# A DeepNorm decoder layer on one core: the gates gb and rg and the two branch projections as seven block products in one stretch, and the rotary tables beside HGRN2

## The chip, the core and the metric

The kernel runs on one core of a Trainium2 chip. The time is that of the device in microseconds (us), from a run of the whole program; lower is better. Before the change the median of three runs is 2408.48 us (2407.49 to 2409.2). The engines of the core are called as the profile calls them: PE is TensorE (PEld its weight loads), DVE is VectorE, ACT is ScalarE, POOL is GpSimd, SP is SyncE, which here only issues transfers (DMAs). POOL issues transfers too, on a queue of its own.

## The reference, cut to what matters

One layer, 1024 tokens of width 1024, everything in float32. `u` is the scaled and shifted input; one wide projection `w_in` gives the inputs of two recurrences and four gates; `rg`, `ga`, `gb` and the projections `w_pa` and `w_pb` are the places of this change.

```python
u = x * (1.0 + scale1) + shift1
hq, hf, hi, hg, rq, rk, rv, rg, ga, gb = jnp.split(u @ w_in[l], split_at, axis=-1)
ya = _hgrn2(hq, hf, hi, hg, lower_bounds[l]) @ w_pa[l]
yb = _retention(rq, rk, rv, rg, positions) @ w_pb[l]
y = (jax.nn.sigmoid(ga) * ya + jax.nn.sigmoid(gb) * yb) @ w_o[l]
x = _layer_norm(DEEPNORM_ALPHA * x + (1.0 + gate1) * y, ln1_g[l], ln1_b[l])
u = x * (1.0 + scale2) + shift2
h = jnp.square(jax.nn.relu(u @ w_up[l] + b_up[l]))
y = h @ w_down[l] + b_down[l]
x = _layer_norm(DEEPNORM_ALPHA * x + (1.0 + gate2) * y, ln2_g[l], ln2_b[l])
...
def _retention(q, k, v, g, positions):
    theta = ROPE_BASE ** (-jnp.linspace(0.0, 1.0, RET_DK // 2, dtype=f32))
    ang = positions.astype(f32)[:, :, None, None] * theta
    cos, sin = jnp.cos(ang), jnp.sin(ang)
    ...
    o = _head_norm(_from_chunks(o), centered=True).reshape(B, S, RET_WIDTH)
    return (o * jax.nn.silu(g.astype(f32))).astype(g.dtype)
```

Here `g` of the retention is `rg` (2048 columns); `gb` and `ga` have 1024 columns, `w_pa` is 1024 x 1024 and `w_pb` 2048 x 1024.

## The kernel before

**Matmuls.** Every float32 operand is split into a high and a low part (`split`, L170 to 172: ScalarE rounds into `wh`, `hh` or `uh`, VectorE subtracts into `wl`, `hl` or `ul`). A product is then three matmuls, `mm3` (L176, L177, L178): high by high, high by low, low by high. Weights come as 512 KB pieces through one stream in the order of a list of specs: SP loads a piece into one of three `raw` tiles, the split writes one of three pairs `wh`, `wl`, two pieces ahead of their use (`W`). SP's queue holds the stream and all other reads in program order, POOL's queue most writes.

**Order of the work.** Start (adaLN, `u` transposed into `uh`, `ul`); HGRN2 in four pairs of heads, each pair's dense projections woven with the recurrence of the one before, outputs stored to `oh_d`; the gate `ga` (to `ga_d`); `h_merge`, which reloads `oh_d`, projects it by `w_pa` and stores the gated result to `y1_d`, woven with `rotary`, which computes the tables of cosines and sines on VectorE and ScalarE; the retention, four heads one after the other (outputs to `or_d`); the gate `gb` (`gate_proj`, to `gb_d`); then for each head of the retention the gate `rg` (`r_merge_gate`: sigmoid, two products with the recurrence's output, split) and its part of the projection by `w_pb` (`r_merge_acc`, which adds into `y`, and for the last head multiplies by gb and adds y1); the output projection, `ffn_up`, `ffn_down`. A scheduler orders the instructions of each engine from this program order and their dependences.

**Seven block products.** `ffn_up` and `ffn_down` already use a form of Strassen's scheme (Winograd's): both matrices are cut into 2 x 2 blocks, and seven products q1 to q7 of sums of blocks replace eight. Sums of weight blocks are made in DRAM by transfers that POOL issues, copies and accumulating copies (`block_sums`, L196 and L197), eight for every part. They are paced by TensorE: `mm3` lets one go each time it has done `PREP` = 40 * 512 columns of matmuls, 42 matmuls of 512 columns (14 calls of `mm3`). Sums of blocks of the other matrix are made by VectorE. For `ffn_down` these are seven variants per tile, written by POOL to `hv_d` (1792 KB a write) and read back by SP into `hr` tiles (512 KB).

Of the kernel before, what the change touches and what calls it, by code (L numbers as in the profile page):

```python
# [58 lines left out]
B12_SLOT = 7  # L59
UP_ORDER = ("q1", "q5", "q6", "q2", "q7", "q3", "q4")  # L60
DN_ORDER = ("q1", "q5", "q6", "q3", "q7", "q2", "q4")
UP_STEPS = ([(q, p) for q in ("q1", "q2") for p in (0, 1)] +
            [(q, p) for p in (0, 1) for q in UP_ORDER if q not in ("q1", "q2")] +
            [(q, p) for p in range(2, 8) for q in UP_ORDER])
LAST = 4
PREP = 40 * 512
# [71 lines left out]
class Trunk:  # L138
# [48 lines left out]
    def block_sums(self, name, w, cut):  # L187


        nc = self.nc  # L190
        kh, nh = w.shape[0] // 2, w.shape[1] // 2
        part = (lambda a, p: a[:, nh // 8 * p:nh // 8 * (p + 1)]) if cut else (lambda a, p: a[kh // 8 * p:kh // 8 * (p + 1), :])
        w11, w12, w21, w22 = ([part(w[k * kh:(k + 1) * kh, n * nh:(n + 1) * nh], p) for p in range(8)]
                              for n in (0, 1) for k in (0, 1))
        s1, s2, s3, s4 = ([self.dp.tile(list(w11[0].shape), F32, name=f"{name}_s{j}_{p}") for p in range(8)] for j in range(1, 5))
        copy = lambda d, a: self.sums.append((0, lambda: nc.gpsimd.dma_start(d, a)))  # L196
        add = lambda late, d, a: self.sums.append((late, lambda: nc.gpsimd.dma_start(d, a, accum_op=ALU.add, max_dma_last_dim=8192)))  # L197
        for p in range(8):
# [103 lines left out]
    def dense_T(self, wh, wl, half, uh=None, ul=None, ks=range(KT), tag="d", k0=0):  # L302
        uh = uh or self.uh
        ul = ul or self.ul
        pd = self.ps(tag)
        sl = slice(half * 512, half * 512 + 512)
        ks = list(ks)
        for k in ks:
            self.mm3(pd, wh[:, k], wl[:, k], uh[k0 + k][:, sl], ul[k0 + k][:, sl], k == ks[0], k == ks[-1])
        return pd  # L310
# [71 lines left out]
    def start(self):  # L382
# [4 lines left out]
        self.uh = [self.up.tile([P, T], F32R, name=f"uh{k}") for k in range(KT)]  # L387
        self.ul = [self.up.tile([P, T], F32R, name=f"ul{k}") for k in range(KT)]
# [41 lines left out]
        def turn(k, hf):  # L430
# [11 lines left out]
            self.split(self.uh[k][:, sl], self.ul[k][:, sl], u32[k][:, sl])  # L442
# [8 lines left out]
        for k in range(KT):  # L451
# [3 lines left out]
            for hf in (0, 1):  # L455
# [4 lines left out]
                sl = slice(hf * 512, hf * 512 + 512)  # L460
                for (wh, wl), bk in zip(wt, banks):
                    self.mm3(bk[hf], wh[:, k], wl[:, k], self.uh[k][:, sl], self.ul[k][:, sl], k == 0, False)
        for j, ((wh, wl), bk) in enumerate(zip(wt, banks)):
            for hf in (0, 1):
                sl = slice(hf * 512, hf * 512 + 512)
                self.mm3(bk[hf], wh[:, k], wl[:, k], self.uh[k][:, sl], self.ul[k][:, sl], False, True)
# [48 lines left out]
    def h_values(self, p):  # L515
# [4 lines left out]
        for t in range(8):  # L520
            pd = self.ps("d", (P, 256))
            for k in range(KT):
                wh, wl = w[k // 4]
                tk = slice(t * P, (t + 1) * P)
                self.mm3(pd, self.uh[k][:, tk], self.ul[k][:, tk], wh[:, k % 4], wl[:, k % 4], k == 0, k == KT - 1)
# [119 lines left out]
    def h_pair_rec(self, p):  # L645
        for hd in (0, 1):
            for _ in self.h_rec(p, hd):
                self.tick()
                yield
# [16 lines left out]


    def h_merge(self):
        nc = self.nc
        oh, ol = [], []  # L670
        for e in range(KT):
            t = self.mp.tile([P, 1024], F32, tag="ohr", bufs=2, name=self.uid("ohr"))
            nc.sync.dma_start(t, self.oh_d[e])
            oh.append(self.mp.tile([P, T], F32R, name=f"oh{e}"))
            ol.append(self.mp.tile([P, T], F32R, name=f"ol{e}"))
            self.split(oh[e], ol[e], t)
        for m in range(KT):
            wh, wl = self.W(("pa", m // 2, m % 2))
            for hf in (0, 1):
                sl = slice(hf * 512, hf * 512 + 512)  # L680
                sg = self.mp.tile([P, 512], F32, tag="sga", bufs=2, name=self.uid("sga"))
                nc.sync.dma_start(sg, self.ga_d[m][:, sl])
                pd = self.dense_T(wh, wl, hf, oh, ol)
                y = self.mp.tile([P, 512], F32, tag="y1", bufs=2, name=self.uid("y1"))
                nc.vector.tensor_tensor(y, pd, sg, op=ALU.mult)
                nc.gpsimd.dma_start(self.y1_d[m][:, sl], y)
                yield


    def rotary(self):  # L690
# [29 lines left out]
        for s in range(T // W):  # L720
            cs = slice(s * W, (s + 1) * W)
            pi = self.rp.tile([P, W], I32, tag="rot_i", bufs=1, name=self.uid("rot"))
            nc.sync.dma_start(pi, self.i["positions"][0:1, cs].to_broadcast([P, W]))
            a, m, y, n = (self.rp.tile([P, W], F32, tag="rot_" + c, bufs=1, name=self.uid("rot")) for c in "amyn")
            V.tensor_copy(a, pi)
# [3 lines left out]
            V.scalar_tensor_tensor(a, m, -65536.0, a, op0=ALU.mult, op1=ALU.add)  # L729
            reduce(a, n)  # L730
            for c in q16[:2]:
                V.tensor_scalar(y, m, sgn * c, None, op0=ALU.mult)
                reduce(y, n)
                V.tensor_tensor(a, a, y, op=ALU.add)
            V.scalar_tensor_tensor(a, m, sgn * q16[2], a, op0=ALU.mult, op1=ALU.add)
            reduce(a, n)
            V.tensor_scalar(a, a, 3.1415925, -3.1415925, op0=ALU.min, op1=ALU.max)
            nc.scalar.activation(self.sin[:, cs], a, AF.Sin)
            nc.scalar.activation(y, a, AF.Sin, scale=0.5)
            V.tensor_tensor(y, y, y, op=ALU.mult)  # L740
            V.tensor_scalar(self.cos[:, cs], y, -2.0, 1.0, op0=ALU.mult, op1=ALU.add)
# [74 lines left out]
    def r_v(self, h, t, w):  # L816
        nc = self.nc
        pd = self.ps("d", (P, 256))
        tk = slice(t * P, (t + 1) * P)
        for k in range(KT):  # L820
            wh, wl = w[k // 4]
            self.mm3(pd, self.uh[k][:, tk], self.ul[k][:, tk], wh[:, k % 4], wl[:, k % 4], k == 0, k == KT - 1)
# [99 lines left out]
    def r_merge_gate(self, h, e, last):  # L922
        nc = self.nc
        wh, wl = self.W(("rg", h, e // 2, e % 2), ahead=0 if last else 1)
        on = self.mp.tile([P, T], F32, tag="onr", bufs=2, name=self.uid("onr"))
        nc.sync.dma_start(on, self.or_d[h][e * P:(e + 1) * P, :])
        oh = self.mp.tile([P, T], F32R, tag="moh", bufs=5, name=self.uid("moh"))
        ol = self.mp.tile([P, T], F32R, tag="mol", bufs=5, name=self.uid("mol"))
        for hf in (0, 1):
            sl = slice(hf * 512, hf * 512 + 512)  # L930
            pd = self.dense_T(wh, wl, hf)
            sg = self.gp.tile([P, 512], F32, tag="gate", bufs=2, name=self.uid("gate"))
            nc.scalar.activation(sg, pd, AF.Sigmoid)
            nc.vector.tensor_tensor(sg, sg, pd, op=ALU.mult)
            nc.vector.tensor_tensor(sg, sg, on[:, sl], op=ALU.mult)
            self.split(oh[:, sl], ol[:, sl], sg)
        return oh, ol

    def r_merge_acc(self, h, mp, os, halves, key, ahead):
        nc, V = self.nc, self.nc.vector  # L940
        wh, wl = self.W(key, k=4, ahead=ahead)
        for j in (0, 1):
            m = 2 * mp + j
            ms = slice(j * P, (j + 1) * P)
            for hf in halves:
                sl = slice(hf * 512, hf * 512 + 512)
                if h == RH - 1:
                    gb = self.mp.tile([P, 512], F32, tag="gbr", bufs=2, name=self.uid("gbr"))
                    nc.sync.dma_start(gb, self.gb_d[m][:, sl])
                    y1 = self.mp.tile([P, 512], F32, tag="y1r", bufs=2, name=self.uid("y1r"))  # L950
                    nc.sync.dma_start(y1, self.y1_d[m][:, sl])
                pd = self.ps("d")
                for e in range(4):
                    self.mm3(pd, wh[:, e, ms], wl[:, e, ms], os[e][0][:, sl], os[e][1][:, sl], e == 0, e == 3)
                ya = self.y[hf][:, m, :]
                if h == 0:
                    nc.scalar.activation(ya, pd, AF.Copy)
                else:
                    V.tensor_tensor(ya, ya, pd, op=ALU.add)
                if h == RH - 1:  # L960
                    V.tensor_tensor(ya, ya, gb, op=ALU.mult)
                    nc.gpsimd.tensor_tensor(ya, ya, y1, op=ALU.add)
# [113 lines left out]
    def variant(self, pool, q, src):  # L1076
        hi, lo = (pool.tile([P, 4, 512], F32R, tag=q + c, bufs=1, name=self.uid(q + c)) for c in "hl")
        for k in (0, 2):
            self.split(hi[:, k:k + 2], lo[:, k:k + 2], src[:, k:k + 2])
        self.act[q] = (hi, lo)  # L1080

    def variants(self, va, vb):

        V = self.nc.vector
# [386 lines left out]
```

## Time and profile before

Times are in us from the start of the profiled span; the columns are the busy times of the engines, the share of the 16 DMA engines and the bytes moved.

| What | time |
|---|---|
| median of three runs | 2408.48 |
| the profiled execution | 2407.94 |
| its span in the profile | 2405.9 |

| Stage | from : to | PE busy | DVE busy | ACT busy | DMA share | GB/s |
|---|---|---|---|---|---|---|
| start | 0 : 60 | 44.52 | 49.12 | 26.82 | 1.01 | 264 |
| HGRN2, end of the first dense part | 60 : 130 | 70.00 | 24.90 | 26.66 | 0.44 | 117 |
| HGRN2, a pair | 250 : 377 | 125.57 | 82.18 | 31.82 | 0.31 | 83 |
| last pair and ga | 505 : 632 | 123.06 | 88.46 | 32.91 | 0.45 | 135 |
| ffn_up | 1810 : 2087 | 277.00 | 137.50 | 157.78 | 0.59 | 204 |
| ffn_down | 2087 : 2406 | 308.50 | 190.88 | 118.25 | 0.63 | 208 |

The stages between 632 and 1810 stand in the prediction. An engine's busy time in a stage, against the stage's length, tells whether it could be the one that sets the pace; the DMA share counts the time that packets took on the 16 engines, so it can exceed 1 where they overlap.

### The profile page before, as it was taken

To read this page: it belongs to the slowest core of one execution; us is meant where nothing else is said; L and a number is where in the kernel's file an instruction comes from. 1 tells how busy PE (TensorE), PEld (TensorE's weight loads), DVE (VectorE), ACT (ScalarE), POOL (GpSimd) and SP (SyncE) were. 2 spreads that over 40 slices of the span, in tenths; PEclk is the share of its full clock that TensorE was granted. 3 is DMA by queue.
4 is the path that set the end of the run, shared out by engine and by line. 5 is a ranking of instruction groups with operands and counts; after the bars stand their busy time and mean duration, and the time that the engine had idled before them with its cause. 6 is when DMAs were issued, how large, how long until landed. Compare 5 with 4: busy or idle time off the path is not lost.

```text
span 2405.9 us, 31784 instructions
## 1 busy us (share of the span) xinstructions
PE 2360.5 (98%) x12434; PEld 2020.3 (84%) x12434; DVE 1383.8 (58%) x2578; ACT 826.5 (34%) x1363; POOL 252.1 (10%) x347
## 2 busy tenths in 40 slices
PE   7999999999999999999999999999999999999998
PEld 5898888887888989898998888887778888888886
DVE  8356667576766474656541324438776454544577
ACT  4322222222312334242432231223366555544332
POOL 0101111112120112111122000003100000000000
PEclk9999999999999999999999999999999999999999
DMA  9324233232875254444446545536424655866673
GB/s 264 104 73 105 62 81 86 80 97 88 242 216 154 54 147 109 123 131 102 131 128 196 154 114 132 140 97 227 158 96 162 215 186 190 298 219 193 212 245 137
DMA packets 223253, 357.65 MB, mean 149 GB/s; under 512 B 12040, under 2 KB 154112, under 8 KB 219008
## 3 DMA queue, kind: packets, MB, share of 16 engines
q1 hardware_dynamic: 186816, 229.32, 30.0%
q0 software_dynamic: 35968, 125.85, 19.5%
q8 instruction: 98, 1.61, 0.3%
q14 instruction: 51, 0.42, 0.1%
q10 hardware_dynamic: 320, 0.45, 0.1%
HBM read 292.65 MB, written 130.03 MB: 176 GB/s over the span
## 4 chain that ended last, share of the span: by engine, by line
PE 90%; DVE 5%; DMA 3%; issue 1%; ACT 1%; POOL 1%; ACTq 0%; SPq 0%; DVEq 0%; POOLq 0%
PE psd L177 22%; PE psd L176 22%; PE psd L178 22%; PE psa L581 3%; PE psb L871 3%; PE psc L176 2%; PE psc L177 2%; PE psc L178 2%; PE psa L177 2%; PE psa L178 2%; PE psa L176 2%; PE psc L858 2%; PE psb L176 1%; PE psb L177 1%; PE psb L178 1%
## 5 line engine op out<-in xcount | busy, mean ns | idle before, releaser
L172 DVE TENSOR_TENSOR wl<-raw,wh 128x512 fp32r<-128x512 f32 (+1 forms) x312 | 294.9, 955 | 325.5 <-ACT wh L171 295.7
L176 PE MATMUL psd<-uh,wh 128*128 128x512 f32 x1128 | 447.1, 397 | 0.0
L177 PE MATMUL psd<-ul,wh 128*128 128x512 f32 x1128 | 444.9, 394 | 0.4 <-DVE ul L172 0.4
L178 PE MATMUL psd<-uh,wl 128*128 128x512 f32 x1128 | 444.0, 394 | 0.0
L171 ACT ACTIVATE wh<-raw 128x512 fp32r<-128x512 f32 (+1 forms) x312 | 259.0, 840 | 493.7 <-PE psd L177 386.2
L177 PEld LDWEIGHTS psd<-ul,wh 128*128 128x128 f32 x1128 | 212.2, 188 | 41.9 <-DVE ul L172 1.5
L178 PEld LDWEIGHTS psd<-uh,wl 128*128 128x128 f32 x1128 | 212.1, 188 | 41.8
L176 PEld LDWEIGHTS psd<-uh,wh 128*128 128x128 f32 x1128 | 211.9, 188 | 41.4 <-ACT uh L171 0.7
L176 PE MATMUL psd<-wh,uh 128*128 128x256 f32 x768 | 221.6, 289 | 0.0
L177 PE MATMUL psd<-wl,uh 128*128 128x256 f32 x768 | 218.2, 284 | 0.0
L178 PE MATMUL psd<-wh,ul 128*128 128x256 f32 x768 | 218.0, 284 | 0.0
L176 PEld LDWEIGHTS psd<-wh,uh 128*128 128x128 f32 x768 | 147.1, 192 | 2.9 <-issue 2.6
L177 PEld LDWEIGHTS psd<-wl,uh 128*128 128x128 f32 x768 | 147.1, 192 | 0.3
L178 PEld LDWEIGHTS psd<-wh,ul 128*128 128x128 f32 x768 | 147.1, 192 | 0.0
L172 DVE TENSOR_TENSOR hl<-hr,hh 128x1024 fp32r<-128x1024 f32 x54 | 66.1, 1223 | 115.7 <-ACT hh L171 115.7
L171 ACT ACTIVATE hh<-hr 128x1024 fp32r<-128x1024 f32 x54 | 57.3, 1061 | 159.8 <-PE psb L177 73.0
L178 PE MATMUL psd<-moh,wl 128*128 128x512 f32 x256 | 99.9, 390 | 1.8 <-DVE wl L172 1.8
L176 PE MATMUL psd<-moh,wh 128*128 128x512 f32 x256 | 99.6, 390 | 0.4 <-ACT wh L171 0.4
L177 PE MATMUL psd<-mol,wh 128*128 128x512 f32 x256 | 99.9, 390 | 0.0
L588 DVE COPY_PREDICATED hS<-mask,psa 128x128 f32<-128x128 uint8 x288 | 77.1, 314 | 31.7 <-PE psa L581 28.9
L827 DVE SCALAR_TENSOR_TENSOR vl<-psd,cst,vh 128x256 fp32r<-128x256 f32 x64 | 30.8, 482 | 82.7 <-ACT vh L826 82.7
L581 PE MATMUL psa<-qp,k 128*128 128x192 f32 x384 | 72.2, 329 | 1.3 <-DVE k L557 1.3
(423 smaller groups left out, 4890.7 us busy)
## 6 DMA issues: line engine op xcount, KB each, us to landing
raw<-in_w_in SPq DMA_DIRECT2D x96, 512.0 KB, 4.3
hv_d<-hv POOLq DMA_DIRECT2D x16, 1792.0 KB, 9.3
hr<-hv_d SPq DMA_DIRECT2D x56, 512.0 KB, 5.5
up_s<-in_w_up POOLq DMA_DIRECT2D x48, 512.0 KB, 5.3
dn_s<-in_w_down POOLq DMA_DIRECT2D x48, 512.0 KB, 5.2
raw<-in_w_ada SPq DMA_DIRECT2D x32, 512.0 KB, 4.5
raw<-up_s SPq DMA_DIRECT2D x32, 512.0 KB, 3.8
raw<-dn_s SPq DMA_DIRECT2D x32, 512.0 KB, 4.7
```

The costliest lines, as they stand in the source:

```text
L171: self.nc.scalar.activation(hi, src, AF.Copy)
L172: self.nc.vector.tensor_tensor(lo, src, hi.bitcast(F32), op=ALU.subtract)
L176: r = mm(out, wh, uh, start=start, stop=False, skip_group_check=more)
L177: mm(out, wh, ul, start=False, stop=False, skip_group_check=more)
L178: l = mm(out, wl, uh, start=False, stop=stop, skip_group_check=more)
L581: nc.tensor.matmul(pa[:, c * 192:(c + 1) * 192].rearrange("p (b w r) -> p b w r", w=2, r=3 * sz), k[:, n * P:(n + 1) * P], mv, start=True, ...
L588: V.copy_predicated(dst, self.mask8[:, o:o + 128].rearrange("p (b two s) -> p b two s", two=2, s=sz), src)
L827: nc.vector.scalar_tensor_tensor(lo, pd, sc, hi.bitcast(F32), op0=ALU.mult, op1=ALU.subtract)
L858: mm(G[e], l[:, n % 2, es], r, start=n == 0 and i == 0, stop=i == 2, skip_group_check=n > 0)
L871: mm(po, l, r, start=i == 0, stop=i == len(pairs) - 1)
```

## The change

**What it does.** The gates gb and rg run as `gates()` right behind the retention, the projections pa and pb behind them as `merge()`, all four in seven block products. `h_merge` is gone from its place ahead of the retention. Their weights take 12 more parts in `block_sums` (2 for gb, 4 for rg, 2 for pa, 4 for pb, besides 8 each for up and dn), so 28 x 8 = 224 sum transfers in place of 128, and `PREP` goes from 40 * 512 to 24 * 512. `u` is kept in four blocks `ub`; `gates()` adds its high and low parts up again (`whole`) and forms the sums of blocks by `t_sums`, which `ffn_up` now shares. The outputs of the recurrences are read into `hv` tiles (`take`: `or_d` for rg, `oh_d` for pa), where rg's gate is multiplied in; their seven variants go by POOL to `av_d` (pa) and `pv_d` (pb) in writes of 1792 KB, and `merge()` reads them as `hr` like `ffn_down` does. The gates ga and gb and the first projection's result y1 are read in pieces of 256 KB (`fetch`). The rotary tables are computed by a generator that is advanced while HGRN2's pairs run, stored to `cos_d` and `sin_d`, and read again ahead of the retention.

```diff
-PREP = 40 * 512
+PREP = 24 * 512
+MERGE_ORDER = ("q1", "q2", "q6", "q7", "q5", "q4", "q3")
+GATE_STEPS = group_steps([("gb", p) for p in range(2)] + [("rg", p) for p in range(4)])
...
+    def product(self, q, name, p):
+
+        wh, wl = self.W((q, name, p), k=4)
+        ah, al = self.act[q]
...
+            for k in range(4):
+                self.mm3(s[tag], wh[:, k, gs], wl[:, k, gs], ah[:, k], al[:, k], first and k == 0, k == 3, not first)
+            yield s, j, s[tag]
...
+    def gate_block(self, s, name, j, n, k, src, sign):
+        nc, V = self.nc, self.nc.vector
+        if name == "gb":
+            r = self.o_tile() if src is s["X"] else src
+            nc.scalar.activation(r, src, AF.Sigmoid, scale=sign)
+            nc.gpsimd.dma_start(self.gb_d[4 * n + j][:, k * 512:k * 512 + 512], r)
+            return
+        r = self.o_tile()
+        nc.scalar.activation(r, src, AF.Sigmoid, scale=sign)
+        V.scalar_tensor_tensor(r, src, sign, r, op0=ALU.mult, op1=ALU.mult)
+        h = s["hv"]
+        d = h[:, BLOCK_SLOT[n, k]]
+        V.tensor_tensor(d, d, r, op=ALU.mult)
+        if (n, k) == (0, 1):
+            self.part_sums(h)
+        elif (n, k) == (1, 0):
+            self.last_sum(h, self.pv_d[j // 2][j % 2])
+
+    def take(self, name, j):
+
+        h = self.fo.tile([P, 8, 512], F32, tag="hv", bufs=2, name=self.uid("hv"))
+        for n, k in BLOCK_SLOT:
+            ks = slice(k * 512, k * 512 + 512)
+            src = self.oh_d[4 * n + j][:, ks] if name == "oh" else self.or_d[2 * n + j // 4][j % 4 * P:j % 4 * P + P, ks]
+            self.nc.sync.dma_start(h[:, BLOCK_SLOT[n, k]], src)
+        return h
+
+    def gates(self, close_r, close_u12):
...
+        for n, (q, name, p) in enumerate(GATE_STEPS):
+            if name == "rg" and q == "q6":
+                for g in (0, 1):
+                    self.grp[name, 2 * p + g]["hv"] = self.take("or", 2 * p + g)
...
+            for s, j, pd in self.product(q, name, p):
+                if n == 0:
+                    for _ in range(6):
+                        self.tick()
...
+                    self.group_out(q, s, name, j, pd, self.gate_block)
+            if n == 0:
+                self.tick(True)
+                close_r()
...
+    def products(self, name, parts, order, banks, z, done, w_moves, hold=0, each=None):
...
+                w = self.W((q, name, p), k=2, ahead=ahead)
+                self.h_split(self.h_base + parts * n + p + (ahead if tail else 2))
...
+                for i in range(4):
+                    mms(q, i, p, w, h)
+                    if p == parts - 1:
+                        finish(q, i)
...
+    def merge(self):
...
+        def fetch(what, src, n, k, i):
+            t = self.mp.tile([P, 512], F32, tag=what, bufs=8, name=self.uid(what))
+            nc.sync.dma_start(t, src[4 * n + i][:, k * 512:k * 512 + 512])
...
+        for name, parts, done in (("pa", 2, done_a), ("pb", 4, done_b)):
...
+            self.products(name, parts, MERGE_ORDER, (b, a), z, done, False, each=each)
...
-    with ExitStack() as s:
-        k.mp = k.pool("hm", "right", s)
-        k.rp = k.mp
-        weave(k.h_merge(), k.rotary(), 16, 4)
+    tc.nc.sync.dma_start(k.cos, k.cos_d)
+    tc.nc.sync.dma_start(k.sin, k.sin_d)
...
+    late, fo = k.gates(rs.close, u12pool.close)
...
+    k.h_begin(42)
...
+        k.merge()
```

**How instructions move.** Three places. The first is SP's queue in the projection pb. Before, where the last head's parts are read (`raw` are weights, `gbr` the gate gb, `y1r` the first projection; `w_pb` and `w_o` are inputs):

```order
253 L264 DMA raw_14866<-in_w_o 128x1024
254 L264 DMA raw_14870<-in_w_pb 128x4x256
255 L949 DMA gbr_14876<-gb_d_93 128x512
256 L951 DMA y1r_14878<-y_d_101 128x512
257 L949 DMA gbr_14896<-gb_d_94 128x512
258 L951 DMA y1r_14898<-y_d_102 128x512
259 L264 DMA raw_14916<-in_w_o 128x1024
260 L264 DMA raw_14920<-in_w_pb 128x4x256
```

And after the change, in the same projection (`hr` are variants of the retention's output, `pv_d` where `gates()` stored them, `g` the gate gb, `y` the first projection):

```order
275 L1092 DMA hr_14103<-pv_d_121 128x2x512
276 L1191 DMA g_14263<-gb_d_93 128x512
277 L275 DMA raw_14048<-in_w_o 128x1024
278 L1092 DMA hr_14138<-pv_d_122 128x2x512
279 L1191 DMA g_14267<-gb_d_94 128x512
280 L1191 DMA g_14271<-gb_d_95 128x512
281 L1191 DMA g_14275<-gb_d_96 128x512
282 L275 DMA raw_14097<-in_w_pb 128x2x512
283 L1092 DMA hr_14175<-pv_d_119 128x2x512
284 L1191 DMA y_2356_14761<-y_d_105 128x512
```

Each weight piece now has an `hr` piece of its size beside it, and the gates' pieces stand among them.

The second place is POOL's queue in the gates (`dn_s` and `up_s` are block sums of the ffn weights, a source `in_w` is an input). Before, in gb:

```order
253 L196 DMA dn_s_4_179<-in_w_down 256x512
254 L663 DMA gb_d_97<-gate_12465 128x512
255 L196 DMA dn_s_4_187<-in_w_down 256x512
256 L663 DMA gb_d_97<-gate_12493 128x512
257 L663 DMA gb_d_98<-gate_12528 128x512
258 L197 DMA dn_s_2_185<-dn_s_2_169 64x2048
259 L663 DMA gb_d_98<-gate_12557 128x512
260 L663 DMA gb_d_99<-gate_12595 128x512
```

After, in rg, between the writes of two parts:

```order
324 L963 DMA pv_d_119<-hv_12344 128x3584
325 L963 DMA pv_d_119<-hv_12349 128x3584
326 L208 DMA up_s_7_198<-up_s_7_190 64x2048
327 L208 DMA dn_s_0_215<-in_w_down 256x512
328 L208 DMA dn_s_0_231<-in_w_down 256x512
329 L207 DMA dn_s_1_216<-in_w_down 256x512
330 L207 DMA dn_s_1_224<-in_w_down 256x512
331 L207 DMA dn_s_1_232<-in_w_down 256x512
332 L207 DMA dn_s_1_240<-in_w_down 256x512
333 L963 DMA pv_d_120<-hv_12637 128x3584
334 L963 DMA pv_d_120<-hv_12642 128x3584
```

Seven sums now stand between two pairs of writes `pv_d`, which did not exist before.

The third place is VectorE's order at the end of the start, where `u` is split for its last two blocks of rows (`ul`) and HGRN2's first tiles (`q`) follow. Before:

```order
169 L172 TENSOR_TENSOR ul_211<-u_6_699,uh_203 128x512
170 L379 SCALAR_TENSOR_TENSOR mod<-psc_299,cols 128x1
171 L172 TENSOR_TENSOR ul_212<-u_7_734,uh_204 128x512 x2
172 L512 TENSOR_TENSOR q_815<-psd_364,sg_816 128x2x256
173 L172 TENSOR_TENSOR wl_776<-raw_253,wh_775 128x512
```

After (`rot` are the rotary tiles):

```order
169 L182 TENSOR_TENSOR ul_261<-u_6_750,uh_260 128x512
170 L386 SCALAR_TENSOR_TENSOR mod<-psc_350,cols 128x1
171 L714 CAST rot_2477<-rot_2478 128x256
172 L715 TENSOR_SCALAR rot_2477<-rot_2477,cst 128x256
173 L716 TENSOR_SCALAR rot_2477<-rot_2477 128x256
174 L717 TENSOR_SCALAR rot_2477<-rot_2477 128x256
175 L718 SCALAR_TENSOR_TENSOR rot_2477<-rot_2477 128x256
176 L182 TENSOR_TENSOR ul_259<-u_7_785,uh_258 128x512
```

The rotary work, which stood at row 964 and behind, beside `h_merge`, now begins ahead of the last split of `u`.

More of the change, by code (lines that the diff above doesn't have):

```diff
@@ L646, in h_pair_rec @@
         for hd in (0, 1):
-            for _ in self.h_rec(p, hd):
+            for n, _ in enumerate(self.h_rec(p, hd)):
                 self.tick()
+                if p in (1, 2) and n % 3 == 1:
+                    next(self.rot, None)
                 yield
@@ L1379, in build @@
     k.hst = {}
+    k.rot = k.rotary()
     with ExitStack() as s:
@@ L1397, in build @@
+    tc.nc.sync.dma_start(k.sin, k.sin_d)
     k.rst = {}
-    with ExitStack() as s:
-        k.rp = k.pool("r", "right", s)
-        for h in range(RH):
-            drain(k.r_head(h))
-        gb = k.gate_proj("gb", k.gb_d)
-        for m in range(4):
-            for j in range(4):
-                next(gb)
-                k.tick()
-        k.tick(True)
-    rot.close()
+    k.rp = k.pool("r", "right", rs)
+    for h in range(RH):
+        drain(k.r_head(h))
+    late, fo = k.gates(rs.close, u12pool.close)
```

639 lines of the change are left out of this document (327 added, 312 removed).

## The prediction

> **What bounds the kernel now.** I read the page first: busy time by engine, the slices, the chain that ended last.
>
> ```profile
> span 2405.9 us, 31784 instructions
> PE 2360.5 (98%) x12434; PEld 2020.3 (84%) x12434; DVE 1383.8 (58%) x2578; ACT 826.5 (34%) x1363; POOL 252.1 (10%) x347
> PE   7999999999999999999999999999999999999998
> DMA  9324233232875254444446545536424655866673
> PE 90%; DVE 5%; DMA 3%; issue 1%; ACT 1%; POOL 1%; ACTq 0%; SPq 0%; DVEq 0%; POOLq 0%
> ```
>
> TensorE is busy for 98% of the span and carries 90% of the chain, so a matmul that goes is worth its full spacing, as long as nothing else in its stage becomes later than TensorE. The DMA row is the second thing to see: it reaches 8 and 9 in places, with TensorE still at 9.
>
> Then I cut the span at the stages. The columns after the engines' busy times are granted clock, DMA share and GB/s.
>
> ```profile
> core 0: us, PE busy (x) PEld busy (x) DVE busy (x) ACT busy (x) POOL busy (x), PEclk, DMA share, GB/s
> 0.00:20.00 20.00, 7.06 (x25) 5.02 (x26) 11.83 (x43) 7.59 (x11) 2.54 (x7) 1.00 1.03 276
> 20.00:40.00 20.00, 18.35 (x92) 13.26 (x90) 18.41 (x67) 9.85 (x15) 0.00 (x0) 1.00 1.12 292
> 632.00:720.00 88.00, 88.00 (x390) 72.87 (x389) 66.10 (x159) 15.98 (x29) 17.85 (x27) 1.00 0.77 216
> 700.00:720.00 20.00, 20.00 (x90) 16.56 (x89) 5.29 (x9) 2.40 (x4) 4.16 (x7) 1.00 0.99 272
> 720.00:1237.00 517.00, 512.32 (x3555) 474.84 (x3553) 309.34 (x646) 174.96 (x369) 69.21 (x102) 1.00 0.43 116
> 1238.00:1330.00 92.00, 92.00 (x426) 76.32 (x425) 13.60 (x27) 22.94 (x41) 22.32 (x34) 1.00 0.67 195
> 1330.00:1440.00 110.00, 110.00 (x486) 90.82 (x485) 35.75 (x50) 34.58 (x56) 8.25 (x12) 1.00 0.46 129
> 1440.00:1550.00 110.00, 110.00 (x487) 90.83 (x486) 48.49 (x68) 25.05 (x38) 8.36 (x12) 1.00 0.49 134
> 1550.00:1634.00 84.00, 84.00 (x372) 69.28 (x371) 35.19 (x51) 16.70 (x26) 4.11 (x5) 1.00 0.40 101
> 1634.00:1681.00 47.00, 44.83 (x195) 35.95 (x194) 41.03 (x44) 17.65 (x18) 18.28 (x12) 1.00 0.80 265
> 1780.00:1810.00 30.00, 27.13 (x111) 21.19 (x110) 24.58 (x27) 21.66 (x34) 1.13 (x2) 0.90 0.28 88
> 2100.00:2120.00 20.00, 20.00 (x90) 16.57 (x89) 8.12 (x7) 8.04 (x8) 0.00 (x0) 1.00 0.90 331
> ```
>
> The work that is changed lies in 632:720 (projection pa) and in 1238:1681 (gb, rg and pb): 88 + 443 = **531 us**, in which TensorE lost about 2 us. There the DMA engines were busy for 0.40 to 0.80, and one 20 us piece, 700:720, shows 0.99 without a stall.
>
> **What the change removes.** Of 2304 matmuls of 512 columns in these four projections an eighth goes: 288. Their price must not be the duration in the row:
>
> ```profile
> L176 PE MATMUL psd<-oh,wh x128: 389/389/389, 632.5 to 718.8; 128*128 128x512 f32 x128
> L178 PE MATMUL psd<-oh,wl x128: 389/389/389, 632.9 to 719.3; 128*128 128x512 f32 x128
> ```
>
> One lasts 389 ns, but these are pipelined: 384 of them (L176, L177, L178) start between 632.5 and 719.3, which is 86.8 us / 383 = 0.2266 us each. So TensorE saves 288 x 0.2266 = **65.3 us**, and the 2016 that stay need 456.8 us. If nothing else were later, the stretch would go from 531 to 457 us plus its seams.
>
> **What it adds: transfers.** Block products of the gates need their inputs combined in DRAM. New or larger traffic in the same stretch, counted from the code and the order: weight pieces of 512 KB, 84 and 8 of w_o; 42 pieces hr of 512 KB; 12 writes av_d and pv_d of 1792 KB; 128 pieces of 256 KB (48 reads of recurrence outputs into hv, 48 reads of ga, gb and y1, 32 writes gb_d and y1_d); and block sums on POOL's queue. These are paced by TensorE's work, one for every 24 matmuls in place of 42: at 0.2266 us, one in 5.4 us, so 2016/24 = 84 fall here. For the prices I take the share that a queue used of the 16 engines over a window, times its length, over the transfers in it; four views, of 130:500, 2120:2406, 1330:1634 and 1810:2087:
>
> ```profile
> q1 hardware_dynamic: 12144, 12.06, 10.6%
> raw<-in_w_in SPq DMA_DIRECT2D x23, 512.0 KB, 3.8
> ...
> q1 hardware_dynamic: 29064, 55.59, 60.0%
> ...
> q0 software_dynamic: 4570, 15.19, 23.1%
> dn_s<-in_w_down POOLq DMA_DIRECT2D x19, 512.0 KB, 5.5
> dn_s<-dn_s POOLq DMA_DIRECT2D x9, 512.0 KB, 5.3
> ...
> q0 software_dynamic: 2016, 25.69, 24.3%
> hv_d<-hv POOLq DMA_DIRECT2D x14, 1792.0 KB, 8.8
> ```
>
> A 512 KB piece in rows of 256 columns: 0.106 x 370 us / 23 = 1.70 us of all engines; in rows of 512 columns (55.59 MB are 106 pieces of 0.524 MB): 0.600 x 286 / 106 = 1.62. A sum: 0.231 x 304 / 29 = 2.42 (the 29th is a write of gb_d). An hv_d write: 0.243 x 277 / 14 = 4.81; av_d and pv_d have its size and layout. For 256 KB I take half of 1.62. Then: 42 pieces of gb and rg x 1.70 = 71; 50 of pa, pb and w_o and 42 hr x 1.62 = 149; 12 x 4.81 = 58; 128 x 0.81 = 104; 84 x 2.42 = 203. Together **585 us of all 16 engines** for 457 us of TensorE: 1.10 of the 531 us that the stretch has now and 1.28 of the 457 us it would like. These prices may hold some waiting of queues against each other; they are then too high, by how much no row shows.
>
> So the question is what share these engines sustain. Rows in which they are the limit: 1.03 and 1.12 at the start, where TensorE waits for weights, 0.99 in 700:720. I take the middle, 1.055: 585 / 1.055 = **554 us**. By bytes: 92 + 42 + 84 pieces of 0.524 MB, 128 of 0.262 and 12 of 1.835 are 170 MB; the busiest rows give 272, 292 and 331 GB/s, so 625, 582 and 514 us. Both ways put it around the 531 us of now, somewhat above.
>
> The Trainium skill speaks against this sum: "Perfetto Trace Analysis", Identifying the Most-Contended Engine, calls occupancy of the 16 DMA engines misleading and asks for bytes, and "DMA: Bandwidth & Descriptors", Specifications, gives 435 GB/s as their ceiling, by which 170 MB would need an estimated 391 us and stay hidden. No 20 us row of this trace comes above 331 GB/s, and at the start, where TensorE waits, 276 and 292 are all there is; so far the rows stand against that figure.
>
> Some of the sums may run late without harm: those of w_down are needed only behind 2087. But they stand in POOL's queue ahead of the writes pv_d, for which the next reads wait; the order shows seven sums between two such pairs. I take 5 us off for the sums still in flight when the merge ends (two landings by the rows above): 549.
>
> **Seams.** At the start of gates() VectorE rebuilds u from its halves and forms the first combinations: per block two additions, two subtractions, two splits, each 128 x 1024.
>
> ```profile
> L172 DVE TENSOR_TENSOR hl<-hr,hh 128x1024 fp32r<-128x1024 f32 x54 | 66.1, 1223 | 115.7 <-ACT hh L171 115.7
> ```
>
> At 1.22 us the ten operations to the first split of q5 are 12 us and those to q6 another 7, behind the last norms of the retention, while the four products q1 and q2 give TensorE 4 x 24 x 0.2266 = 21.8 us. The same seam of the up projection (1780:1810, no rebuilding) lost 2.9 us. Bounds 0 to 10; I take 3, since a stretch limited by transfers uses the pause in part.
>
> **VectorE in rg.** A part p of 7 weight pieces lasts 38.1 us of TensorE; VectorE has 7 splits of 1.22 and 30 operations of 128 x 512:
>
> ```profile
> L935 DVE TENSOR_TENSOR gate<-gate,onr x32: 684/692/693, 1336.4 to 1638.4; 128x512 f32<-128x512 f32 x32
> ```
>
> 8.6 + 30 x 0.69 = 29.3 us, 77% of it, against 44% in 1440:1550. It fits; cost 0, up to 5 where a bank waits for its reader.
>
> **Rotary tables.** VectorE's part was hidden beside pa; it is mainly this group:
>
> ```profile
> L718 DVE SCALAR_TENSOR_TENSOR rot<-rot,rot 128x256 f32<-128x256 f32 x64 | 27.2, 424 | 2.0
> L738 ACT ACT_TABLE_LOAD x1 | 1.3, 1283 | 0.0
> 60.00:130.00 70.00, 70.00 (x404) 61.78 (x403) 24.90 (x42) 26.66 (x47) 7.37 (x11) 1.00 0.44 117
> ```
>
> The order puts it between the last splits of u and the first pair, where VectorE is busy for only 25 of 70 us; eight more table loads on ScalarE (10.3 us) find idle time too. The first operations stand ahead of the splits of u for k = 7, for which TensorE waits, and wait themselves for the load of positions: cost 1 us, bounds 0 and 4. Were that load to come late, its whole delay would count. The tables' reload before the retention (2 x 512 KB) lies beside the ga projection of 30 us: 0.
>
> **HGRN2 and retention.** Sums come 42/24 = 1.75 times as often; the retention's DMA share 0.43 would become about 0.55, where TensorE already loses 4.7 of 517 us. Nearest rows: 0.67 to 0.99 with no stall. 1 us, bounds 0 and 4. The output projection and both ffn stages keep their order: 0.
>
> **Sum.** 2405.9 - 531 + 549 + 3 + 1 + 1 = 2428.9 us of span. The profiled execution took 2407.94, 2.04 more than its span, so **2431 us**; that execution lies 0.5 us below the median of 2408.48.
>
> **The rivals.**
>
> *A, the forecast: the DMA engines become the bound* in the stretch, at a share of 1.00 to 1.10 (532 to 585 us, less 5 for late sums): 2405.9 - 531 + 527 to 580 + 5 + 2, that is 2409 to 2462. For it: the counts, and 1.03 at the start. Against it: the first 40 us also wait for small loads, so they may not be a full test. Chance 0.50.
>
> *B, the other side: faster.* The mechanism is that packets of several rings overlap, so that the engines do more than one unit of work per unit of time, as 1.12 in 20:40 shows, or that my prices hold waiting that falls away. The point that decides is a sustained share of 1.10: from there the stretch is shorter than 531 us. At 1.15 it takes 509 us: 2405.9 - 531 + 509 + 5 + 2 = 2391. If the transfers hide wholly, TensorE is the bound: 2405.9 - 531 + 456.8 + 10 + 2 = 2344. For it: TensorE did not stall at 0.99, nor at 331 GB/s in 2100:2120. Against it: these last 20 us, and the new need lasts 457. By the skill's 435 GB/s, "DMA: Bandwidth & Descriptors", Specifications, 2344 would be the result. Chance 0.35, with most weight at 2360 to 2400.
>
> *C, a chain of landings.* In rg each part's hv tiles go out by POOL, land, and their two buffers are refilled by SP, which holds the weight loads behind it meanwhile:
>
> ```profile
> hv_d<-hv POOLq DMA_DIRECT2D x16, 1792.0 KB, 9.3
> hr<-hv_d SPq DMA_DIRECT2D x56, 512.0 KB, 5.5
> up_s<-up_s POOLq DMA_DIRECT2D x2, 512.0 KB, 8.6
> ```
>
> 9.3 us unloaded, 1.6 times that if it grows as a sum's landing did in 700:720 (8.6 against 5.3): 15, and the read behind it 5.5 to 9. That is 15 to 24 us against the 22 us (four pieces) between a part's last sum and the next part's first use, so 0 to 10 us per part, on top of A: 2445 to 2475. Chance 0.15.
>
> *The change does not do what it says*: the rotary work comes earlier than beside the last pairs, by the order. It is worth the 0 to 4 us above and decides no sign, so it has no chance of its own.
>
> **How the numbers follow.** Two per mille, 4.8 us, is about what a measurement of this kernel can tell from no change. A's 0.50 lies slower but for 0.06 within it and 0.02 faster, where its prices are too high; B's 0.35 is faster but for 0.05 within; C's 0.15 is slower. Faster 0.32, same 0.11, slower 0.42 + 0.15 = 0.57. A's own range is 2409 to 2462; to hold 8 in 10 the range goes down into B to 2370, which leaves about 0.10 below, and up to 2470.
>
> **What would show it.** In the new profile: a DMA share near 1 from about 1240 to 1790 with TensorE at 80 to 85% there, waiting for raw or hr (A right); a share near 1 or above and TensorE at 95% or more (B); POOL's pv_d and the reads into hv as the longest waits of the stretch, share under 0.95 (C). The seam should show about 3 us idle before the first q5 and q6 matmuls, the start not more than 4 us later. The prediction is wrong if landings of raw stay near 4 us at a share above 1, since then transfers wait for nothing.

## The result, and the profile after

The changed kernel takes 2480.3 us (median of four runs, 2476.64 to 2485.1) against 2408.64 before: a ratio of 1.0299, with a 95% interval of 1.028 to 1.0318. It is slower, as forecast, but by 72 us where 22 were forecast, and outside the stated range.

The page of the changed kernel, its lines that answer to those shown of before:

```profile
span 2477.1 us, 31812 instructions
PE 2335.1 (94%) x12146; PEld 1984.7 (80%) x12146; DVE 1493.4 (60%) x2680; ACT 909.3 (37%) x1425; POOL 313.9 (13%) x447
PE   7989999999999999999878879899899999999998
PEclk9999999999999999999989989999999999999999
DMA  9544444444755655555798889999424556676674
PE 73%; DMA 11%; DVE 7%; issue 6%; ACT 1%; POOL 1%; SPq 1%; ACTq 0%; DVEq 0%; POOLq 0%
```

TensorE has 288 matmuls less, yet the span grew, and its share of the chain fell from 90 to 73%: transfers, VectorE and issue have come between. The 40 slices show where: in the second half, PE drops to 7 and 8 and the granted clock to 8 where the DMA row stands at 8 and 9. The stages, cut at their first and last matmuls (the rows are gates, merge, output projection; the last three columns are clock, DMA share, GB/s):

```profile
1162.00:1478.00 316.00, 254.98 (x1045) 203.79 (x1043) 170.11 (x223) 102.40 (x143) 53.23 (x79) 0.91 0.85 262
1478.00:1741.00 263.00, 241.25 (x1008) 195.46 (x1008) 148.84 (x160) 104.43 (x116) 39.71 (x59) 0.95 1.03 340
1741.00:1852.00 111.00, 100.09 (x433) 78.90 (x434) 70.61 (x104) 36.55 (x65) 7.38 (x13) 0.97 0.27 94
```

Gates and merge hold 1008 matmuls of 512 columns each, 228.4 us at 0.2266. The gates lose 61 us to waits (316 less the busy 255) and (1 - 0.91) x 316 = 28 us to a lower clock: 228 + 61 + 28 = 317. The merge loses 22 and 13. Together they take 579 us where the same work took 531 before. The output projection took 96.3 us before (1681.2 to 1777.5) and takes 111, 14.7 more. Between the start and the retention's first scores another 11 us are lost; the retention itself takes 481 us in both kernels, and the two ffn stages are 3.5 us shorter together.

### The profile page after: what moved, and what is told of

The parts are those of the page before. It is cut to its first block, busy times and chain, and to the rows that moved or that the text cites. A ratio compares the mean times of both kernels' runs of the same rounds, so it can differ in the third digit from the quotient of the medians.

```text
span 2477.1 us, 31812 instructions
## 1 busy us (share of the span) xinstructions
PE 2335.1 (94%) x12146; PEld 1984.7 (80%) x12146; DVE 1493.4 (60%) x2680; ACT 909.3 (37%) x1425; POOL 313.9 (13%) x447
## 4 chain that ended last, share of the span: by engine, by line
PE 73%; DMA 11%; DVE 7%; issue 6%; ACT 1%; POOL 1%; SPq 1%; ACTq 0%; DVEq 0%; POOLq 0%
PE psd L188 15%; PE psd L186 15%; PE psd L187 15%; PE psc L186 3%; PE psc L187 3%; PE psc L188 3%; PE psa L590 3%; PE psb L866 2%; PE psa L186 2%; PE psa L187 2%; PE psa L188 2%; PE psc L853 2%; DMA hv<-or_d 1%; DMA raw<-in_w_ada 1%; DVE wl L182 1%
## 5 line engine op out<-in xcount | busy, mean ns | idle before, releaser
L182 DVE TENSOR_TENSOR wl<-raw,wh 128x1024 fp32r<-128x1024 f32 (+1 forms) x312 | 327.8, 1056 | 315.3 <-ACT wh L181 304.5
L181 ACT ACTIVATE wh<-raw 128x1024 fp32r<-128x1024 f32 (+1 forms) x312 | 287.4, 928 | 471.9 <-PE psd L187 210.7
L186 PE MATMUL psd<-uh,wh 128*128 128x512 f32 x788 | 317.3, 404 | 6.7 <-DVE o L1015 6.7
L187 PE MATMUL psd<-ul,wh 128*128 128x512 f32 x788 | 314.9, 400 | 0.4 <-DVE ul L182 0.4
L188 PE MATMUL psd<-uh,wl 128*128 128x512 f32 x788 | 313.8, 398 | 0.0
L186 PEld LDWEIGHTS psd<-uh,wh 128*128 128x128 f32 x788 | 149.3, 190 | 36.5 <-DVE o L1015 8.0
L187 PEld LDWEIGHTS psd<-ul,wh 128*128 128x128 f32 x788 | 149.7, 190 | 28.7 <-DVE ul L182 1.3
L188 PEld LDWEIGHTS psd<-uh,wl 128*128 128x128 f32 x788 | 149.4, 190 | 28.9 <-DVE wl L182 0.2
L597 DVE COPY_PREDICATED hS<-mask,psa 128x128 f32<-128x128 uint8 x288 | 76.9, 314 | 27.3 <-PE psa L590 24.5
L590 PEld LDWEIGHTS psa<-qp,k 128*128 128x128 f32 x384 | 62.1, 189 | 11.3 <-issue 7.4
L188 PE MATMUL psd<-wh,hl 128*128 128x512 f32 x168 | 65.4, 389 | 0.0
```

The costliest lines, as they stand in the source:

```text
L181: self.nc.scalar.activation(hi, src, AF.Copy)
L182: self.nc.vector.tensor_tensor(lo, src, hi.bitcast(F32), op=ALU.subtract)
L186: r = mm(out, wh, uh, start=start, stop=False, skip_group_check=more)
L187: mm(out, wh, ul, start=False, stop=False, skip_group_check=more)
L188: l = mm(out, wl, uh, start=False, stop=stop, skip_group_check=more)
L590: nc.tensor.matmul(pa[:, c * 192:(c + 1) * 192].rearrange("p (b w r) -> p b w r", w=2, r=3 * sz), k[:, n * P:(n + 1) * P], mv, start=True, ...
```

## The experiments

All start from the changed kernel. The first six were run once each, the last four four times each; the kernel before took 2409.16 us in the session of the rotary, cap, `PREP` 15 and later-product runs, and 2407.03 (median of seven) in that of the two others. The changed kernel's own four runs spread over 8.5 us, so a difference of some 10 us in a single run is read together with the stage that it comes from.

**Rotary work later.** The start of each quarter's load waits for a matmul of the pair in which the code places it.

```diff
-        l = mm(out, wl, uh, start=False, stop=stop, skip_group_check=more)
+        l = self.last = mm(out, wl, uh, start=False, stop=stop, skip_group_check=more)
...
-            nc.sync.dma_start(y.bitcast(I32), self.i["positions"][0:1, cs].to_broadcast([P, W]))
+            self.after(nc.sync.dma_start(y.bitcast(I32), self.i["positions"][0:1, cs].to_broadcast([P, W])), self.last)
```

> The load of positions for each quarter of the rotary tables waits for the matmul issued last at its place in the program, so the rotary work starts in the second and third pair of HGRN2 instead of ahead of the first. Theory (VectorE's rotary work delayed the first pair by 7.3 us, and TensorE then ran 6.8 us at half clock): 10 us less, 2470, with no TensorE wait over 1.5 us between 60 and 640. Rival (the stretch of gates and merge sets the end by its transfers, and an earlier arrival only waits longer there): 2478 to 2482.

Measured: 2470.08, 10 us less. The window 60:250, first of the changed kernel, then of this one:

```profile
60.00:250.00 190.00, 181.39 (x1040) 159.32 (x1039) 145.17 (x368) 67.24 (x118) 31.09 (x42) 0.98 0.48 124
```

```profile
60.00:250.00 190.00, 189.24 (x1098) 166.47 (x1097) 101.10 (x231) 57.55 (x110) 27.94 (x37) 1.00 0.46 120
```

44 us of VectorE's work leave the window, TensorE's busy time rises by 8 us, its clock goes back to 1.00, and 58 more matmuls start in it. The wait behind the rotary work was this row of the changed kernel (waits of TensorE, same place: total, times, longest):

```profile
PE psa L554 <- DVE hS L558: 7.3, 1, 7.3
```

With the later rotary work no wait of TensorE between 60 and 640 is longer than 1.2 us, and the theory holds.

**The stream capped at the end of pb.**

```diff
+                if name == "pb":
+                    ahead = min(ahead, 27 - (parts * n + p))
                 w = self.W((q, name, p), k=2, ahead=ahead)
```

> The stream splits no weight of ffn_up ahead of the end of projection pb. Theory (those two pieces hold two of the three wh/wl pairs through the output projection, so its inputs yh/yl, which use the same pairs, have one buffer): the output projection falls from 111 us to 97 to 100 us, 2467 to 2470 in all. Rival (y itself is complete too late): at most 3 us less, 2477 or more.

Measured: 2459.27, 21 us less, and more than expected: the output projection takes 92 us, 4 less than before the change. In the changed kernel its inputs `yh` wait for TensorE to give a buffer free; the first row is its wait view (ScalarE, 1741:1860), the second the capped kernel's window:

```profile
ACT yh L181 <- PE psd L187: 56.8, 7, 16.1
```

```profile
1741.00:1833.00 92.00, 92.00 (x431) 76.57 (x430) 70.72 (x105) 37.45 (x65) 7.96 (x14) 1.00 0.37 129
```

Seven of the eight `yh` were made only when the last use of the one before was over. ScalarE's wait alone is no loss: the capped kernel still has 30.1 us of it. The loss is that TensorE in turn waited for `yl`, which it does not in the capped kernel, where it is busy for 92.00 of 92 us instead of 100.09 of 111. TensorE's wait in the changed kernel (1741:1860):

```profile
PE psd L188 <- DVE yl L182: 9.2, 8, 3.6
```

The code of before asked for 0 pieces ahead at the end (`0 if final else 2`); the new general function asks for 2 always.

**All sums ahead of the gates.** `PREP` 24 to 15.

> One block sum for every 15 matmuls, so all 224 are issued ahead of gates(). Theory A (transfers are the bound in merge, share 1.03): merge falls from 263 us to 235, gates from 316 to 285 as landings get shorter, HGRN2 and retention lose up to 10: 2425 to 2435. Rival C (waits in the order of the queues are the bound, whatever the share): merge and gates fall by less than 15 us together, 2465 or more. If the 140 us of sums merely stall the earlier stages, those grow by what the stretch gains: 2480.

Measured: 2402.45, 78 us less, one and a half times what theory A had said. The stages gates and merge of this kernel:

```profile
1181.00:1434.00 253.00, 237.80 (x1049) 194.01 (x1048) 171.20 (x224) 104.42 (x143) 21.82 (x37) 0.97 0.68 241
1434.00:1665.00 231.00, 230.25 (x1008) 190.17 (x1008) 147.74 (x160) 103.75 (x116) 9.18 (x17) 0.99 0.84 293
```

The merge comes to 231 us, 2.6 above its matmuls' own time, at a share of 0.84; the gates to 253. Same matmuls, same weights, same variants: only the 84 sums are gone from these stages. The retention pays 15 us (496) and HGRN2 5; the output projection stays at 111. Rival C as this expectation puts it, waits whatever the share, is refuted: gates and merge lose 95 us, not under 15. Theory A had the merge right (235 expected, 231 measured) and the gates wrong (285 expected, 253 measured).

**First product in rg later.**

```diff
-                    self.group_out(q, s, name, j, pd, self.gate_block)
+                    self.group_out(q, s, name, j, pd, self.gate_block, defer=name == "rg")
```

> In rg the first product with a recurrence output is made after q7 instead of after q2, 5.4 us later, with the same reads and writes. Theory C (VectorE waits in its order for the reads into hv, and PSUM banks of TensorE behind it): VectorE's wait for hv falls from 27 us to under 10, gates lose 15 to 25 us: 2455 to 2465. Rival A (transfers alone): 2478 to 2482, the waits move to weights.

Measured: 2471.69, 9 us less; the gates take 305 us, 11 less, and VectorE's wait for reads into `hv` falls less than expected. VectorE's waits in the gates (1160:1480), first of the changed kernel, then of this one:

```profile
DVE hv L957 <- DMA hv<-oh_d: 37.0, 4, 13.4
DVE hv L1018 <- DMA hv<-or_d: 27.3, 6, 6.8
```

```profile
DVE hv L957 <- DMA hv<-oh_d: 37.7, 4, 13.9
DVE hv L1018 <- DMA hv<-or_d: 19.6, 6, 7.3
```

The chain that theory C names exists, but 5.4 us more do not break it, and its largest part is the other read, that of HGRN2's outputs for pa. No run moved that read, or the sums made from it, to another place in VectorE's order.

**Reads into hv by POOL.**

```diff
-            self.nc.sync.dma_start(h[:, BLOCK_SLOT[n, k]], src)
+            self.nc.gpsimd.dma_start(h[:, BLOCK_SLOT[n, k]], src)
```

> The reads into hv are issued by POOL instead of SP, so the weight loads no longer stand behind a read that waits for av_d or pv_d to land (43 us of SP's time in gates); the transfers are the same. If that order is what costs: gates 290 to 300, 2455 to 2465. If the transfers' amount is what costs: 2475 to 2490, and block sums are issued later.

Measured: 2450.87, 29 us less; both expectations were off, the one by 4 us, the other by more. The gates take 288 us at a **higher** DMA share:

```profile
1161.00:1449.00 288.00, 243.65 (x1048) 196.69 (x1046) 171.68 (x224) 102.91 (x143) 79.64 (x127) 0.95 0.92 291
```

The 42 sums of the gates are issued in them as before, and the bytes moved are the same. In the changed kernel SP's queue waits in the gates (1160:1480) at the reads into `hv` (L1030) until a write has landed, with the weight loads behind it:

```profile
SPq L1030 <- DMA av_d<-hv: 27.2, 4, 12.8
SPq L1030 <- DMA pv_d<-hv: 15.6, 5, 4.3
```

With POOL as the issuer these waits leave SP's queue, and VectorE's waits for the reads shrink:

```profile
DVE hv L957 <- DMA hv<-oh_d: 24.1, 3, 18.0
DVE hv L1018 <- DMA hv<-or_d: 4.3, 3, 2.2
```

So in the gates the order of SP's queue decided about a third of the loss of 89 us. The edit also moves the reads from one kind of queue to another (q1 to q0 in the page's terms), which this run cannot separate from the order.

**No sums during the gates alone.** Pacing stops ahead of `gates()` and goes on with the merge.

```diff
+    k.paced = False
     late, fo = k.gates(rs.close, u12pool.close)
+    k.paced, k.cols_done = True, 0
```

> The changed kernel with no block sum issued while gates() runs; the same pacing before it and from the merge on, so that the 42 sums of the gates fall into the output projection and ffn_up. If the sums are what gates lose time to: gates 250 to 258 instead of 317, merge unchanged at 260 to 265 with its own sums, 2480 - 62 = 2418. If the loss of the gates is the reads' order (SP's queue behind the writes av_d and pv_d): gates stay over 295 and the time over 2455.

Measured: 2419.58 (before 2407.03 beside it), as expected to 2 us. Gates and merge:

```profile
1164.00:1414.00 250.00, 236.19 (x1045) 193.34 (x1045) 170.84 (x223) 105.08 (x143) 21.30 (x37) 0.98 0.69 243
1414.00:1677.00 263.00, 241.27 (x1008) 194.39 (x1008) 148.04 (x160) 103.83 (x115) 40.01 (x59) 0.95 1.03 338
```

The two stages are independent: the gates fall to 250, the merge stays at its 263 and 1.03. That sums stand in POOL's queue ahead of the writes `pv_d` cost nothing in the changed kernel's gates: each of the seven writes issued there starts 0.3 us after VectorE's last sum for it.

**Versions that beat both.** The first combines `PREP` 15, the cap and the later rotary work:

> The earlier pacing (one sum for 15 matmuls), the cap on the stream at the end of pb and the later rotary work together. If the three losses are separate, their gains add: 2402.5 - 18 - 9 = 2375 (2370 to 2380), 1.4% below the kernel before the change. If the gain of the cap came only from transfers of ffn_up that had competed with the merge's, it shrinks here, where the merge has room: 2385 or more.

2381.28 (ratio 0.9892, 0.9867 to 0.9916): 1 us outside the stated range and some 10 us above what the three measured gains give when added. The output projection takes 92 us, so the cap keeps its gain; the retention is again at 496, and why the sum is not reached stays open. The next holds sums back: one for 20 matmuls up to the retention's end, none in gates and merge, the rest in the output projection and ffn_up, with the cap, the rotary edit and the later product in rg. (Sums are let go after whole calls of `mm3`, so with matmuls of 512 columns 20 means 21, and 14 below means 15.)

```diff
-PREP = 24 * 512
+PREP = 20 * 512
...
-        if self.paced and self.cols_done >= PREP:
+        if self.paced and self.cols_done >= self.pace * 512:
...
+    k.paced = False
     late, fo = k.gates(rs.close, u12pool.close)
...
         k.merge()
     hsp.close()
+    k.paced, k.pace, k.cols_done = True, 24, 0
```

> One sum for 20 matmuls up to the retention's end, none during gates and merge, the rest (the sums of w_down) one for 24 in the output projection and ffn_up; with the cap, the later rotary work and the later first product in rg. Theory A (what counts is how much transfer falls into one stage): gates 240 to 250 and merge 231 as with the early pacing, the retention 485 instead of 496, ffn_up 312 to 316 although a fifth more transfers fall there, since it stood at 0.56: 2355 to 2370. Rival (ffn_up's bursts at 0.99 leave no room): ffn_up 325 or more and 2375 to 2385.

2373.32 (0.9853, 0.9836 to 0.9869), between the two ranges: 3 us above theory A's and 2 below the rival's. Theory A holds for the merge (231) and within 2 us for gates (252) and ffn_up (317), but the retention takes 492 instead of 485. So the third spaces the sums as the change did before the gates (24), then 14 and 20:

> As the held-back version, but one sum for 24 matmuls up to the retention's end, and the rest one for 14 in the output projection and one for 20 in ffn_up. If the retention's 492 us came from the closer pacing: 481 to 484, ffn_up 316 to 322, 2362 to 2370. If from the other edits: 490 or more and 2373 to 2380.

2365.45 (0.983, 0.9813 to 0.9846), as expected, with the retention at 485, 1 us outside its range: the closer pacing had cost it. Its stages from the retention to ffn_up:

```profile
672.00:1157.00 485.00, 477.90 (x3396) 446.31 (x3395) 287.00 (x606) 167.75 (x354) 86.80 (x122) 0.99 0.55 142
1157.00:1409.00 252.00, 238.18 (x1048) 194.01 (x1046) 169.86 (x223) 104.33 (x143) 21.81 (x37) 0.98 0.69 242
1409.00:1640.00 231.00, 230.68 (x1007) 190.67 (x1008) 147.73 (x159) 103.18 (x115) 9.19 (x17) 0.99 0.83 289
1640.00:1734.00 94.00, 92.76 (x435) 77.04 (x434) 70.27 (x106) 37.35 (x65) 27.39 (x39) 1.00 0.93 249
1734.00:2052.00 318.00, 310.89 (x1361) 255.61 (x1360) 161.00 (x192) 178.92 (x256) 51.33 (x76) 0.99 0.95 287
```

The output projection and ffn_up run at shares of 0.93 and 0.95, and TensorE is idle in them for 1 and 7 us, where it was idle for 61 in the gates of the changed kernel at 0.85. The last window took 312 us in the changed kernel (1852 to 2164, share 0.56), so the sums moved into it cost some 6 us. With POOL as the issuer of the reads into `hv` on top:

> The best version so far (held-back sums, one for 24 matmuls before gates) with the reads into hv issued by POOL as well. If the order of SP's queue costs only while sums compete for the transfers (gates without sums had no wait for hv left): gates stay at 250 to 252, 2362 to 2368. If the order costs by itself: gates 235 to 242, 2350 to 2356.

2364.1 (0.9823, 0.9804 to 0.9842), gates 250: without sums beside them, the order of SP's queue costs nothing that can be told apart. All four versions gain less than 2% on the kernel before, though each interval lies below 1. A third `hv` buffer was not tried.

## Why the prediction was right in sign and wrong in size

The forecast span was 2428.9, the measured one is 2477.1: 48 us short. Of these 27 are in the stretch of gates and merge, 14.7 in the output projection and 10 ahead of the retention, less 3.5 in the two ffn stages. By its own steps:

- **288 matmuls, 65.3 us.** Right: where nothing interferes the merge takes 231 us for 1008 matmuls, 0.229 each.
- **The DMA engines become the bound: 549 us and 3 for the seam.** 579, so 27 us short. In the merge the step was right: share 1.03, 263 us, back to 231 without the sums. The amount of work was somewhat overpriced: 0.85 x 316 + 1.03 x 263 = 540 us of the engines instead of 585. What failed is the sustained share, 1.055 assumed for the whole stretch: the gates reached 0.85, so the mean is 0.93. At a share of 1.03 the gates' own 269 us of work would have needed 261 us, not 316. Their load comes unevenly: pieces of 20 us stand at 0.42 (1182:1202) and at 1.10 (1282:1302). With sums beside them the landings are longer, 10.3 us in place of 7.3 for the reads `hv<-or_d` where POOL issues them (with the sums in the run of the reads by POOL, without in the last version), and reads and writes that wait for each other in the order of SP's, VectorE's and TensorE's instructions turned this into waits.
- **Rival C** named this kind of wait, priced at 0 to 10 us for each part on top of A and given 0.15; A in the merge and waits like C's in the gates came true together. But C's own chain is not what grew. It had a write `pv_d` landing in 15 us; the median in the gates is 8.2, and 7.5 in the run with all sums ahead of the gates. In that run SP's queue waits for `pv_d` 16.6 us, as long as with the sums (15.6). What grew against it is the wait for `av_d`, the outputs for pa (27.2 us, there 14.8), and VectorE's waits for the reads into `hv` (37.0 and 27.3 us, there 17.4 and 1.8). The runs show the share of each cause as far as they go: no sums alone (gates 250), another queue alone (288), a later product alone (305). What of the rest falls to which wait stays open.
- **The seam, 3 us.** Too small. Two waits of TensorE, 1.6 and 4.9 us long, stand at q6, with a low clock behind them. With no sums at all the gates still take 250 to 253 us against 228 of matmuls and some transposes: besides these two waits there is one of 5 to 6 us for the merge's first hr, and a clock of 0.97 to 0.98. No run took these away.
- **The output projection, 0.** Wrong by 14.7 us. "Keep their order" overlooked that the stream ahead of it had changed: two pieces of ffn_up held two of three buffers that its inputs use. The capped run shows it.
- **Rotary tables, 1 us (0 to 4).** 10 us. The place was right, and the idle time of VectorE was there, but on average: the work stood ahead of the first pair's instructions just when TensorE waited for them.
- **HGRN2 and retention, 1 us.** About right: the retention takes 481 us in both kernels, and of the 11 us lost ahead of it the rotary run took 10 away.
- **What was left out: a wait costs more than its length.** The prediction's working shows the row 1780:1810 with a clock of 0.90 and counts only its 2.9 us of idle time. In the gates and the merge the clock takes 28 + 13 us, half of what the waits themselves take (61 + 22).

So the result lies in the direction of A, beyond it through waits of C's kind, and the point on which B rested, a sustained share of 1.10, did not occur: the merge held 1.03 over 263 us, the gates 0.85. The 435 GB/s of the Trainium skill ("DMA: Bandwidth & Descriptors", Specifications) were not reached either: 340 GB/s in the merge, where the engines were the limit. Whether their own pace sets it or that of the memory behind them, no run separates; the share counts the time of packets in both cases. The sign that the prediction named for being wrong, landings of `raw` near 4 us, could not be read: the profile of the changed kernel gives no landing time for these loads.

## What to carry to other kernels

Where work is exchanged for transfers, ask not only how much falls into a stage but what waits for it: background transfers that nobody waits for cost some 6 us in a stage of 318 at a share of 0.95, while reads with a deadline lost 89 of 316 us at 0.85. Move the background traffic to the stages that have no deadline, and count a wait of TensorE of about 3 us or more at nearly one and a half times its length (61 us of waits and 28 of clock in the gates). When a special case is folded into a general function, look for what its exceptions ("0 ahead at the end") had protected.

## What the runs showed of the hardware

TensorE's clock falls to a half behind a wait, for several us. In the gates and the merge of the changed kernel this follows each of the eleven waits of 3.3 us or more (3.36 to 10.56), at once or within about 1 us, for some 3 to 6 us. Of five waits between 2.4 and 2.9 us it follows three (2.43 and twice 2.70) and not the others (2.48 and 2.84). The timeline of the changed kernel in the gates (start, duration, instruction, then the idle time before it and what ended it):

```profile
1271.77 0.80 PE L186 MATMUL psd<-q4h,wh 128*128 128x512 f32 x1 [10.56 <-DVE o L996]
1272.36 0.63 PE L187 MATMUL psd<-q4l,wh 128*128 128x512 f32 x1
1272.79 0.63 PE L188 MATMUL psd<-q4h,wl 128*128 128x512 f32 x1
...
1276.14 0.40 PE L188 MATMUL psd<-q4h,wl 128*128 128x512 f32 x1
1276.37 0.39 PE L186 MATMUL psb<-q4h,wh 128*128 128x512 f32 x1
```

And what VectorE did then:

```profile
1270.42 0.69 DVE L957 TENSOR_TENSOR hv<-hv 128x512 f32<-128x512 f32 x1 [13.42 <-DMA hv<-oh_d]
1271.03 0.68 DVE L996 TENSOR_TENSOR o<-o,psd 128x512 f32<-128x512 f32 x1
```

VectorE stands 13.42 us at a read that belongs to a later stage (pa), with the reader of a PSUM bank (the place of TensorE's results) behind it in its order; TensorE waits 10.56 us for that bank; then its matmuls start 0.43 us apart instead of 0.23 until 1275.7. The Trainium skill, "TensorE: Matmul & The Clock Gate", section "HAM oscillation — how this bites in real kernels", describes this: a wait for a transfer drops the clock to one half, and the next work starts slow, each time anew. The trace agrees, with clocks of 0.91 and 0.95 over the two stages; here TensorE's wait is for VectorE, which waits for the transfer.

The second is the price of accumulating transfers. In DRAM, a copy of 512 KB and a sum of the same size move the same counted bytes. The queue of POOL in two windows of 9.5 us of the kernel before, the first with one copy (1421.7:1431.2), the second with one sum of an input (1402.7:1412.2):

```profile
q0 software_dynamic: 144, 0.52, 16.8%
...
q0 software_dynamic: 272, 0.52, 36.6%
```

These are 1.6 and 3.5 us of all engines. SP's queue moves more beside the second, but that is not the reason: in two windows where it moves next to nothing the shares of POOL's queue are 17.7% (a copy, 1507.5:1517) and 35.5% (a sum of an input, 1412.2:1421.7). Counted bytes alone say nothing of that.
